# RMSNorm on one core: four of the first loads issued by ScalarE instead of SyncE, and gamma loaded in one piece

## The chip, the cores and the metric

The kernel runs on one core of a Trainium2 chip. The metric is the device time of one execution in microseconds (us). The core has a matrix engine (TensorE), three engines for elementwise work (VectorE, ScalarE, GpSimd), SyncE, which here only issues transfers, and sixteen DMA engines that move data between the chip's main memory (HBM) and the on-chip memory (SBUF). An engine that issues a transfer puts it on its own DMA queue; the sixteen DMA engines then work through it. In the profile PE is TensorE, DVE VectorE, ACT ScalarE, POOL GpSimd and SP SyncE; a q behind the name means its instruction queue.

## The reference

Each of 16 x 1024 rows of 512 float32 numbers is divided by its root mean square and multiplied by a vector gamma.

```python
def reference(x, gamma):          # x: 16 x 1024 x 512, gamma: 512, float32
    eps = 1e-5
    rms = np.sqrt(np.mean(x ** 2, axis=-1, keepdims=True) + eps)
    return (x / rms * gamma).astype(np.float32)
```

33.5 MB are read and 33.5 MB written.

## The kernel before

The 16384 rows are cut into four tiles t = 0 to 3. A tile has 128 partitions of 32 rows each; one row of a partition is 2 KB, so one row index over all partitions is 256 KB. Three buffers of a whole tile, slot 0 to 2 (line 40), hold tiles 0, 1, 2 and again slot 0 for tile 3. Results are written over the inputs in the slot and stored from there.

The work goes by nine groups of rows (line 76), each with a count of rows that GpSimd takes. For a group, ScalarE squares the rows (line 96) and VectorE adds the squares along each row (line 97), in pieces of up to nine rows. ScalarE takes the root of the mean (line 102) and VectorE its reciprocal (line 103). Then ScalarE multiplies the rows by the reciprocal one at a time (line 118) and VectorE multiplies them all by gamma (line 122); GpSimd does both steps for its own rows (lines 109 and 110). The loop of line 168 issues the squares of the next group ahead of the scaling of this one.

Gamma is loaded as one row of 512 numbers into one partition (line 58) and spread over the 128 partitions by a matmul with a column of ones (line 66). VectorE reads the product from TensorE's memory (PSUM); ScalarE copies it to SBUF for GpSimd (line 167), once, behind the reciprocals of the first group.

The schedule is written out by hand: each engine executes its instructions in the order of the program. Before the change every transfer is issued by SyncE, and so stands in one queue. The order at the start is: row 0 of tile 0 (line 55), rows 1 to 7 (line 56), gamma in five pieces (lines 57 and 58), rows 8 to 15, rows 16 to 31 (lines 59 and 60), and rows 0 to 15 of tile 1 (line 61). All the other transfers are issued in `transfers` (line 129), each group's at the end of its turn of the loop, so a store there waits for VectorE's product with gamma and for GpSimd's. The first of these is the store of row 0 after the first group.

The first group is the seven rows 0 to 6, so the first Square needs the first two loads. Completion of transfers is signalled on eight semaphores that are used in turn: the ninth transfer waits until the first one has landed, the tenth until the second one has, and so on. Before the change, rows 0 to 15 of tile 1 are the tenth transfer, and wait for rows 1 to 7 of tile 0.

ScalarE's instructions begin with an alignment of its code (line 34, in the trace a branch), then the load of the table for Sqrt and one Sqrt of a small constant (line 72), and then the Square of the first group.

## Time and profile before

| | before |
|---|---|
| median of 3 runs | 161.44 us (161.40 to 161.46) |
| the profiled execution | 161.45 us |
| its span, from the first to the last instruction | 159.7 us |
| busy: VectorE, ScalarE, GpSimd, TensorE | 112.0, 107.8, 106.4, 2.0 us |
| bytes read and written | 33.56 and 33.55 MB |
| first Square (line 96) | starts at 8.19 us |
| last product with gamma (line 122) | 131.92 us, 7.09 us long |

The times inside the span count from its first instruction. A busy time is the sum of an engine's instructions, without its issues of transfers and its waits. "Landing" is the moment when a transfer's completion has been signalled. In the windows, a row gives the stretch and its length in us, then the busy time of PE, PEld, DVE, ACT and POOL with the number of instructions, the granted clock of TensorE, the mean busy share of the sixteen DMA engines and what they moved in GB/s; a packet counts in the stretch in which it starts, so a single short stretch can show more than the engines can move.

### The profile page before, as it was taken

The numbers are of one execution on the slowest core, as the hardware profiler recorded it, in microseconds if no ns is written. First come the engines' busy times: TensorE is split into PE (matmuls) and PEld (weight loads), VectorE is DVE, ScalarE is ACT, GpSimd is POOL, SyncE is SP. The second block draws the span as 40 slices with busy tenths as digits, with TensorE's granted clock in tenths as the row PEclk, the third lists the DMA queues.
The fourth block names the chain that finished last, engine by engine and source line by source line (L and its number), as shares of the span: only waits on it lengthen the run. The fifth ranks groups of instructions, "written<-read, shape, count | busy, mean of one in ns | idle before, by whom it ended". The sixth has DMA issues, their size and how long they took to land.

```text
span 159.7 us, 276 instructions
## 1 busy us (share of the span) xinstructions
PE 2.0 (1%) x2; PEld 0.5 (0%) x2; DVE 112.0 (70%) x39; ACT 107.8 (68%) x108; POOL 106.4 (67%) x24
## 2 busy tenths in 40 slices
PE   0050000000000000000000000000000000000000
PEld 0010000000000000000000000000000000000000
DVE  0018098899798999999999999999999009800000
ACT  3071967976999999999899999989960990000000
POOL 1000951994999599999999999999999990000000
DMA  5999999999989989898999999979996997999995
GB/s 190 424 435 464 460 394 435 355 458 451 460 378 543 401 345 460 378 517 345 443 468 394 460 394 525 509 318 445 509 517 263 525 460 328 394 435 484 394 419 238
DMA packets 2747, 67.12 MB, mean 420 GB/s; under 512 B 313, under 2 KB 314, under 8 KB 826
## 3 DMA queue, kind: packets, MB, share of 16 engines
q1 hardware_dynamic: 2746, 67.11, 98.2%
q14 instruction: 1, 0.01, 0.0%
HBM read 33.56 MB, written 33.55 MB: 420 GB/s over the span
## 4 chain that ended last, share of the span: by engine, by line
DVE 59%; ACT 22%; DMA 4%; ACTq 0%; issue 0%; SPq 0%
DVE ss L97 36%; DVE slot L122 23%; ACT slot L118 8%; ACT slot L96 7%; ACT sq_psum L96 6%; DMA slot<-in_x_dram 4%; DVE ss L103 1%; ACT ss L102 1%; ACTq L210 0%; ACT gamma_b L167 0%; SPq L45 0%; ACTq L96 0%
## 5 line engine op out<-in xcount | busy, mean ns | idle before, releaser
L109 POOL TENSOR_TENSOR slot<-slot,ss 128x3584 f32<-128x3584 f32 (+2 forms) x9 | 46.9, 5214 | 24.0 <-DVE ss L103 24.0
L110 POOL TENSOR_TENSOR slot<-slot,gamma_b 128x3584 f32<-128x3584 f32 (+2 forms) x9 | 59.2, 6582 | 0.7
L97 DVE TENSOR_REDUCE ss<-sq_psum 128x7 f32<-128x3584 f32 (+1 forms) x13 | 42.2, 3246 | 13.5 <-ACT sq_psum L96 13.5
L118 ACT ACTIVATE slot<-slot,ss 128x512 f32<-128x512 f32 x75 | 47.2, 706 | 4.7 <-DVE ss L103 4.7
L122 DVE TENSOR_TENSOR slot<-slot,gamma_psum 128x4608 f32<-128x4608 f32 (+2 forms) x9 | 41.3, 4590 | 8.7 <-ACT slot L118 8.7
L96 ACT ACTIVATE sq_psum<-slot 128x3584 f32<-128x3584 f32 (+1 forms) x13 | 34.5, 2656 | 6.2 <-DMA slot<-in_x_dram 5.5
L97 DVE TENSOR_REDUCE ss<-slot 128x9 f32<-128x4608 f32 x3 | 14.9, 4953 | 4.4 <-ACT slot L96 4.2
L97 DVE TENSOR_REDUCE ss<-sq_sbuf 128x5 f32<-128x2560 f32 x5 | 14.0, 2801 | 0.0
L96 ACT ACTIVATE slot<-slot 128x4608 f32<-128x4608 f32 x3 | 12.1, 4033 | 0.0
L96 ACT ACTIVATE sq_sbuf<-slot 128x2560 f32<-128x2560 f32 x5 | 11.6, 2324 | 0.4 <-DMA slot<-in_x_dram 0.4
L102 ACT ACTIVATE ss<-ss,eps_t 128x16 f32<-128x16 f32 (+2 forms) x9 | 2.7, 304 | 11.6 <-DVE ss L97 11.6
L103 DVE RECIPROCAL ss<-ss 128x16 f32<-128x16 f32 (+2 forms) x9 | 2.1, 235 | 0.4 <-ACT ss L102 0.4
L66 PE MATMUL gamma_psum<-gamma_row,ones_col 1*128 1x512 f32 x2 | 2.0, 1122 | 8.7 <-DMA gamma_row<-in_gamma_dram 8.7
L72 ACT ACT_TABLE_LOAD x1 | 1.3, 1283 | 1.2 <-PEq L199 1.2
L167 ACT COPY gamma_b<-gamma_psum 128x512 f32<-128x512 f32 x1 | 0.6, 567 | 0.0
L66 PEld LDWEIGHTS gamma_psum<-gamma_row,ones_col 1*128 1x128 f32 x2 | 0.5, 304 | 8.7 <-issue 8.7
L64 POOL MEMSET ones_col<- 1x128 f32 x1 | 0.2, 194 | 0.3 <-POOLq L199 0.3
L199 POOL MEMSET const-float32-0.0<- 128x1 f32 x1 | 0.1, 99 | 0.2 <-issue 0.2
L72 ACT ACTIVATE table<-eps_t 128x1 f32<-128x1 f32 x1 | 0.2, 202 | 0.0
L199 POOL MEMSET const-bfloat16-1.0<- 128x1 bf16 x1 | 0.1, 102 | 0.0
L199 POOL MEMSET const-uint8-127<- 128x1 uint8 x1 | 0.1, 102 | 0.0
L199 POOL MEMSET const-float32-1.0<- 128x1 f32 x1 | 0.1, 99 | 0.0
(1 smaller groups left out, 0.1 us busy)
## 6 DMA issues: line engine op xcount, KB each, us to landing
slot<-in_x_dram SPq DMA_DIRECT2D x5, 4096.0 KB, 24.7
out_dram<-slot SPq DMA_DIRECT2D x3, 4096.0 KB, 20.3
out_dram<-slot SPq DMA_DIRECT2D x1, 7936.0 KB
slot<-in_x_dram SPq DMA_DIRECT2D x1, 5888.0 KB
out_dram<-slot SPq DMA_DIRECT2D x1, 3584.0 KB
slot<-in_x_dram SPq DMA_DIRECT2D x1, 2304.0 KB, 25.8
slot<-in_x_dram SPq DMA_DIRECT2D x1, 2048.0 KB, 9.8
slot<-in_x_dram SPq DMA_DIRECT2D x1, 1792.0 KB, 6.9
```

What stands on the lines that cost most here:

```text
L66: nc.tensor.matmul(gamma_psum[:, 0], ones_col, gamma_row, start=True, stop=True)
L72: nc.scalar.activation(out=table, in_=eps_t, func=AF.Sqrt)
L96: nc.scalar.activation(out=sq[:, :m], in_=rows, func=AF.Square)
L97: nc.vector.tensor_reduce(out=ss[:, r : r + m, 0], in_=sq[:, :m], axis=mybir.AxisListType.X, op=OP.add)
L102: nc.scalar.activation(out=ss[:, :n, 0], in_=ss[:, :n, 0], func=AF.Sqrt, bias=eps_t, scale=1.0 / D)
L103: nc.vector.reciprocal(out=ss[:, :n, 0], in_=ss[:, :n, 0])
L109: nc.gpsimd.tensor_tensor(out=part, in0=part, in1=by_row, op=OP.mult)
L110: last = nc.gpsimd.tensor_tensor(out=part, in0=part, in1=gamma_b.to_broadcast([P, share, D]), op=OP.mult)
L118: nc.scalar.activation(out=x[:, g + r, :], in_=x[:, g + r, :], func=AF.Copy, scale=rstd[:, r])
L122: scaled = nc.vector.tensor_tensor(out=part, in0=part, in1=gamma_psum.to_broadcast([P, r1 - r0, D]), op=OP.mult)
L167: nc.scalar.copy(out=gamma_b[:, 0], in_=gamma_psum[:, 0])
L199: nc = _bacc.Bacc("TRN2", target_bir_lowering=False, num_devices=1)
```

## The change

The load of the first row stays on SyncE. Rows 1 to 7, 8 to 15 and 16 to 31 of tile 0 and rows 0 to 15 of tile 1 are issued by ScalarE on its own queue, in that order, behind the alignment of line 34 and ahead of its table load. Gamma is one transfer of 2 KB on SyncE, behind the first row. All later transfers, and all compute instructions, stay where they are. With four transfers fewer, the turn of the eight semaphores shifts for all the later ones.

```diff
-    def load(t, slot, r0, r1):
-        dma = nc.sync.dma_start(out=slots[slot][:, r0:r1], in_=xv[t][:, r0:r1])
+    def load(t, slot, r0, r1, queue=nc.sync):
+        dma = queue.dma_start(out=slots[slot][:, r0:r1], in_=xv[t][:, r0:r1])
         before_scale.append((slot, r0, r1, dma))
...
     gamma_row = const.tile([1, D], fp32)
-    pieces = (0, 128, 224, 320, 416, D)
-
     load(0, 0, 0, 1)
-    load(0, 0, 1, 8)
-    for c0, c1 in zip(pieces, pieces[1:]):
-        nc.sync.dma_start(out=gamma_row[:, c0:c1], in_=gamma.unsqueeze(0)[:, c0:c1])
-    load(0, 0, 8, 16)
-    load(0, 0, 16, 32)
-    load(1, 1, 0, 16)
+    load(0, 0, 1, 8, nc.scalar)
+    nc.sync.dma_start(out=gamma_row, in_=gamma.unsqueeze(0))
+    load(0, 0, 8, 16, nc.scalar)
+    load(0, 0, 16, 32, nc.scalar)
+    load(1, 1, 0, 16, nc.scalar)
```

## The prediction, as it stood before the result

> **What bounds the kernel now.** I read the page's DMA rows first, then the chain, then SyncE's timeline, and last the DMA issues one at a time, because the first two rows contradict each other. The chain of the page:

> ```profile
> DVE 59%; ACT 22%; DMA 4%; ACTq 0%; issue 0%; SPq 0%
> ```

> By this the end is set by VectorE and ScalarE. But the DMA rows of the same page say that the transfers had no time left over:

> ```profile
> DMA  5999999999989989898999999979996997999995
> ...
> q1 hardware_dynamic: 2746, 67.11, 98.2%
> ...
> HBM read 33.56 MB, written 33.55 MB: 420 GB/s over the span
> ```

> All 67.11 MB go through one queue, and its packets took 98.2% of the sixteen engines' span. Whether the chain or the queue sets the end is told by SyncE's timeline, which lists when each transfer was issued:

> ```profile
> 0.74 0.86 SPq L45 DMA_DIRECT2D slot<-in_x_dram  x2
> 1.65 1.48 SPq L58 DMA_DIRECT2D gamma_row<-in_gamma_dram  x5
> 3.17 5.28 SPq L45 DMA_DIRECT2D slot<-in_x_dram  x3
> 27.23 0.35 SPq L49 DMA_DIRECT2D out_dram<-slot  x1
> ...
> 83.50 55.90 SPq L49 DMA_DIRECT2D out_dram<-slot  x4
> ```

> and by the DMA issues of single stretches (around 1.2, 8.1 and 139.1 us), each with its size and its time from issue to landing:

> ```profile
> slot<-in_x_dram SPq DMA_DIRECT2D x1, 1792.0 KB, 6.9
> ```
> ```profile
> slot<-in_x_dram SPq DMA_DIRECT2D x1, 4096.0 KB, 24.7
> ```
> ```profile
> out_dram<-slot SPq DMA_DIRECT2D x1, 4096.0 KB, 19.8
> ```

> The last one is the last store, issued at 139.1 when VectorE ended; it lands 19.8 us later. Its 4.19 MB need 9.8 us at the 426 GB/s that the windows give for 8 us to the end. So some 10 us of other transfers were still ahead of it: VectorE could have ended up to about 9 us later without moving the end. The chain only follows the last issue back to whoever released it and doesn't see the transfers queued ahead. The same holds at every place where SyncE waits for compute. The tightest is the first: the store issued at 27.23 finds ahead of it the load that was issued at 8.1 and lands 24.7 us later, at 32.8, so with the 1.0 us from an issue to its first bytes (first issue 0.74; the window 0 to 1.75 moved nothing) it came some 4.5 us early. **The end is set by the start of the first transfer plus 67.11 MB at the rate of the queue.** Only three things can move it: when the bytes start, how full the engines are in the first microseconds, and the rate. The windows show the start:

> ```profile
> 0.00:1.75 1.75, 0.00 (x0) 0.00 (x0) 0.00 (x0) 0.59 (x1) 0.43 (x6) 1.00 0.00 0
> 1.75:4.00 2.25, 0.00 (x0) 0.00 (x0) 0.00 (x0) 0.89 (x2) 0.00 (x0) 1.00 1.02 337
> 4.00:8.00 4.00, 0.00 (x0) 0.00 (x0) 0.00 (x0) 0.00 (x0) 0.00 (x0) 1.00 1.01 423
> 8.00:159.70 151.70, 2.04 (x2) 0.49 (x2) 112.04 (x39) 106.32 (x106) 105.95 (x18) 1.00 0.99 426
> ```

> The last two columns are the DMA share and GB/s: nothing until 1.75, 337 GB/s until 4.0, from there 423 to 426. The loss in the ramp is 2.25 x (1 - 337/426) = 0.47 us.

> The sum is made against the profiled execution's own 161.45 us: a span of 159.7 and 1.75 around it. The median of the runs is 161.44, so nothing need be corrected. A measurement of this kernel can tell about 0.2%, 0.32 us, from no change.

> **The change, part by part.** I call the five loads L1 (one row, 256 KB), L2 (seven rows), L3, L4 and L5.

> *L1 stays first on SyncE*: same place, 0.74. Its first bytes still come at 1.75. Cost 0.

> *L2 moves to ScalarE.* Before, SyncE issued it second: a first issue of 0.38 us (the chain's piece at 0.74), so L2 stood at 1.18. Now it is ScalarE's first work, behind the branch of line 34 that aligns its code. How early ScalarE can issue is read from its timeline:

> ```profile
> 1.16 1.28 ACT L72 ACT_TABLE_LOAD   x1 [1.16 <-PEq L199]
> ```

> ScalarE's first instruction behind that branch stands at 1.16 though the branch itself is at 0.73 and 33 ns long. In the built order of the changed kernel the four DMA copies stand behind the branch and ahead of this table load, so L2's issue takes its slot: 1.16 in place of 1.18, a gain of 0.02 us. Bounds: no earlier than 0.74 (SyncE's first issue after the same barrier), which would be 0.44 earlier; at the late end behind something as long as the table load, at 2.45. I take 1.16, since it is the same slot on the same engine.
> [...]

> But even an earlier L2 gains only what the engines are idle. L1's 256 KB take 0.62 us at 426 GB/s, so from 1.75 it keeps them busy until at least 2.37; L2 is needed there, which with 1.0 us from issue to bytes means an issue by 1.36. At 1.16 it has 0.2 us to spare. What L2 can do if it comes in beside L1 is fill the ramp: at most the 0.47 us above, at least nothing. I take 0.03: an L2 that is as early as before finds the same ramp.

> *L3, L4 and L5* follow on ScalarE, at 0.37 us each (the median of the ten issues of line 45, 0.33 to 0.60), about 1.6, 2.0 and 2.5. Before: 3.17, 3.66 and 8.1, the last of them held until L2 had landed, by the turn of eight DMA semaphores. They queue behind L2, which lands at 8.1, so an earlier issue moves no byte: 0.

> *ScalarE's compute behind them*: four issues of about 0.43 with their gaps put the table load at 2.9 in place of 1.16, its end and the small Sqrt at 4.4. The first Square waits for L1 and L2 until 8.19, which hides 3.8 us; even with all four at 0.60 it is hidden. If that cover were gone, each microsecond would delay the first store, which has its 4.5 us: 0.

> *SyncE*: one gamma issue for five saves some 1.2 us of an engine that then waits until 27.2: 0. Gamma lands earlier, TensorE's matmul (8.70) may start earlier, but the copy of its result stands at 15.52 behind VectorE's sums: 0. On the DMA engines gamma is 2 KB of 67 MB. The turn of semaphores shifts by four; each later issue of SyncE then waits on transfers that had landed at least 9 us before by the order of the queue, or on the same data as before: 0.

> *Two queues beside each other.* From 28.2 to 32.8 SyncE's store and loads run beside the rest of L5 on ScalarE's queue, where before they stood behind it. The bytes are the same. If the two share evenly, L5 lands between 32.8 and 37.4 (twice the 4.6 us left); its first reader, the Square at 37.69, takes it either way. Whether the rate changes is not shown by a one-queue trace: the window 28 to 32 has 349 GB/s against 426 in the 14 us before, some 0.7 us short, and the 22 us after it have 453 and pay it back. So between a gain and a loss of 0.7; I take 0, the rate over both stretches (437).

> Sum: 161.45 - 0.02 - 0.03 = **161.4 us**.

> **The rivals.**
> *Faster: the ramp is filled.* ScalarE issues L2 nearer to 0.74 and its long packets keep the engines full while L1's short ones start. For it: both engines pass the barrier together, and 337 GB/s is well below 426. Against it: 1.16, and L1's bytes are in the way. All of the ramp gives 161.45 - 0.47 = 161.0; it counts as faster from two thirds on.

> *Slower: L2 comes late.* It is ScalarE's first DMA, right behind a branch after which its next instruction took 0.39 us to come (0.76 to 1.16). If the first issue costs such a stop once more (1.55) and takes 0.60, the longest issue of line 45, in place of 0.38, it is 0.39 + 0.22 = 0.61 later. The engines run dry from a delay of 0.2 on (1.16 to 1.36), and each microsecond beyond costs one: 161.45 + 0.41 = 161.9. At the far end (2.45) it is 1.1, 162.5. For it: ScalarE has issued no DMA in this trace, so its price is unknown. Against it: four or five slots of SyncE, all under 0.6.

> *Slower as well, less likely: the shared stretch.* Two queues lower the rate at 28 to 33 by up to 0.7: 162.1. And the same with the other sign, 160.8.

> That the change doesn't do what it says is excluded: the built order shows the four copies ahead of ScalarE's table load, and a single gamma transfer.

> **How the numbers follow.** No change, 161.4, has 0.62: the end hangs on bytes, and none is added or taken away. Its own range is 161.13 to 161.76. The faster cases have 0.18 (ramp 0.13, shared stretch 0.05), the slower ones 0.20 (late L2 0.14, shared stretch 0.06). The range of 8 in 10 takes in the ramp rival and the late L2 at 0.41, and leaves out the far ends: 160.95 to 162.0.

> **What would show it.** L2's issue on ScalarE's queue near 1.16, and 337 GB/s or so in 1.75 to 4.0: step right; an issue at 0.8 and over 400 GB/s is the ramp rival, an issue after 1.4 and a hole in the window 2 to 3 the late one. The table load near 2.9 with the first Square still near 8.2; L5 landing before 37.4; the last store still landing some 19 us after an issue near 139. What would make it wrong: a DMA share well under 98%, or a last store that finds the queue empty, since then the chain and not the queue would set the end.

## The result and the profile after

The changed kernel takes **163.37 us** (median of 4 runs, 163.27 to 163.46) against 161.44: a ratio of 1.0103 over the runs that were compared (95% interval 1.0069 to 1.0138; the two medians alone give 1.0120). I had forecast 161.4 with a range up to 162.0. The profiled execution takes 163.30 with a span of 161.5, that is 1.85 more than that of the kernel before.

The loss sits at both ends of the span. First the start, in the timeline of the changed kernel (start, length, engine and line, what):

```profile
0.73 0.38 SPq L45 DMA_DIRECT2D slot<-in_x_dram  x1
...
1.17 0.31 SPq L55 DMA_DIRECT2D gamma_row<-in_gamma_dram  x1
1.17 3.73 ACTq L45 DMA_DIRECT2D slot<-in_x_dram  x4
3.28 0.50 PEld L63 LDWEIGHTS gamma_psum<-gamma_row,ones_col 1*128 1x128 f32 x2 [3.28 <-issue]
...
4.93 1.28 ACT L69 ACT_TABLE_LOAD   x1 [4.93 <-issue]
6.22 0.20 ACT L69 ACTIVATE table<-eps_t 128x1 f32<-128x1 f32 x1
9.71 3.16 ACT L93 ACTIVATE sq_psum<-slot 128x3584 f32<-128x3584 f32 x1 [3.28 <-DMA slot<-in_x_dram]
```

ScalarE starts to issue at 1.17, as forecast, but its four issues take 3.73 us and not 1.7. The answer for line 45 alone (shortest, median and longest in ns) says which:

```profile
L45 SPq DMA_DIRECT2D slot<-in_x_dram x6: 328/401/570, 0.7 to 77.7; - x6
L45 ACTq DMA_DIRECT2D slot<-in_x_dram x4: 448/506/2182, 1.2 to 4.3; - x4
```

One issue took 2182 ns, and the trace shows it to be the first, L2, from 1.17 to 3.35. With the 0.63 us from the end of an issue to its first bytes (before: 1.12 to 1.75) L2's bytes begin at 3.98. L1's end at 3.18, so the sixteen engines run empty. The windows of the changed kernel show it against 337 and 423 GB/s before:

```profile
1.75:4.00 2.25, 0.69 (x1) 0.50 (x2) 0.00 (x0) 0.00 (x0) 0.00 (x0) 1.00 0.51 133
4.00:8.00 4.00, 1.36 (x2) 0.00 (x0) 0.00 (x0) 1.49 (x2) 0.00 (x0) 1.00 0.98 355
8.00:28.00 20.00, 0.00 (x0) 0.00 (x0) 10.52 (x4) 11.76 (x10) 6.19 (x2) 1.00 1.02 439
```

2.25 x (337 - 133) + 4 x (423 - 355) = 731 KB fewer, 1.7 us at 426 GB/s (the bins count a packet where it starts, so this is good to a tenth or two). By the column with the DMA share, 2.25 x (1.02 - 0.51) + 4 x (1.01 - 0.98) = 1.27 us of it are engines that stand idle. The rest is a second ramp: from 4 to 8 us they are as busy as before, at 355 GB/s. From 8 us on the rate is what it was (438 before), and every later landing is 1.6 later: L5 at 34.4 in place of 32.8, the last store at 140.6 + 19.8 = 160.4 in place of 139.07 + 19.8 = 158.9:

```profile
out_dram<-slot SPq DMA_DIRECT2D x1, 4096.0 KB, 19.8
```

The other 0.25 us lie behind the last landing, in SyncE's checks of the semaphores. The same answer for the last line of the program, before and after:

```profile
L210 SPq EVENT_SEMAPHORE  x7: 17/28/28, 139.5 to 159.6; - x7
```
```profile
L207 SPq EVENT_SEMAPHORE  x7: 17/28/28, 160.5 to 161.5; - x7
```

Before, SyncE made its first checks at 139.5, while the last store was still moving, and the last of the five at 158.86 was the one that waited for it. After, the first check is the one that waits (until 160.45), and the other four follow behind the last landing, 62 ns apart. From the last landing to the end of the span it is 1.08 us in place of 0.83. So 1.60 + 0.25 = 1.85, all of the difference.

The rest went as forecast: two queues appear, and gamma's matmul starts at 3.3 in place of 8.7 without effect.

```profile
q1 hardware_dynamic: 2162, 54.79, 79.0%
q10 hardware_dynamic: 576, 12.32, 18.3%
```

### The profile page after: what moved, and what is told of

It reads as the page before. It is cut to its first block, busy times and chain, and to the rows that moved or that the text cites. A ratio compares the mean times of both kernels' runs of the same rounds, so it can differ in the third digit from the quotient of the medians.

```text
span 161.5 us, 270 instructions
## 1 busy us (share of the span) xinstructions
PE 2.0 (1%) x2; PEld 0.5 (0%) x2; DVE 112.0 (69%) x39; ACT 107.8 (67%) x108; POOL 106.4 (66%) x24
## 3 DMA queue, kind: packets, MB, share of 16 engines
HBM read 33.56 MB, written 33.55 MB: 416 GB/s over the span
## 4 chain that ended last, share of the span: by engine, by line
DVE 58%; ACT 22%; DMA 5%; issue 0%; ACTq 0%
DVE ss L94 35%; DVE slot L119 23%; ACT slot L115 8%; ACT slot L93 7%; ACT sq_psum L93 6%; DMA slot<-in_x_dram 5%; DVE ss L100 1%; ACT ss L99 1%; ACTq L207 0%; ACT gamma_b L164 0%; ACTq L34 0%
## 5 line engine op out<-in xcount | busy, mean ns | idle before, releaser
L93 ACT ACTIVATE sq_psum<-slot 128x3584 f32<-128x3584 f32 (+1 forms) x13 | 34.5, 2657 | 3.9 <-DMA slot<-in_x_dram 3.3
## 6 DMA issues: line engine op xcount, KB each, us to landing
slot<-in_x_dram SPq DMA_DIRECT2D x3, 4096.0 KB, 24.9
out_dram<-slot SPq DMA_DIRECT2D x3, 4096.0 KB, 20.4
slot<-in_x_dram ACTq DMA_DIRECT2D x2, 4096.0 KB, 25.2
```

What stands on the lines that cost most here:

```text
L93: nc.scalar.activation(out=sq[:, :m], in_=rows, func=AF.Square)
```

## The experiments

Theory: the first issue by ScalarE is slow, which empties the engines, and the turn of the semaphores leaves four more checks behind the last landing. Open at first were why that issue is slow, and how much of the loss is the queue's start and how much the first Square, 1.5 us later. The runs of some kernels spread over 2 us, as do a few of the kernel before (161.34 to 163.72 in these comparisons); where that matters I say where most lie.

**e1, L2 back on SyncE.**

```diff
-    load(0, 0, 1, 8, nc.scalar)
+    load(0, 0, 1, 8)
```

> The changed kernel, with the second load (rows 1 to 7) back on SyncE; the next three loads stay on ScalarE, gamma stays one piece. Theory 'first issue': ScalarE's first issue of a transfer takes 2.2 us whatever it carries, and cost the changed kernel its start because the second load hung on it. Here it falls on the load of rows 8 to 15, whose bytes are not wanted before 7.3, so the start is as before (first Square near 8.2) and only the end's 0.25 stays: 161.45 + 0.25 = 161.7. Rival 'two queues': the rate falls while two queues share the engines; then most of the loss stays, about 163. Rival 'shape': the seven-row load is slow to issue on ScalarE; then ScalarE's first issue is about 0.45 here, and the time 161.7 too.

Median 163.13, ratio 1.0052 (1.0010 to 1.0093). Five of twelve runs lie at 161.8 to 162.0, the others at 163.0 to 163.8 but for one at 165.0, and the profile (163.81) is one of those. Its first ScalarE issue, now L3, takes 2237 ns again, so it is not the shape of L2. Its start is not quite that of before: L3 shares the engines with L2 from 4.0 on, so L2 lands at 9.65 and the first Square starts at 9.74. The lower group fits the theory. In the profile of the upper one SyncE's issue behind the first store is long, and at 32.5 only 8 of the 16 engines are busy; e14 to e16 look into this. The group may not be e1's alone: 7 of the 23 runs of the kernel before beside it lie at 162.3 to 163.3 too, and none of those was traced.

```profile
29.19 2.81 SPq L45 DMA_DIRECT2D slot<-in_x_dram  x1
```

**e2, gamma in one piece, all on SyncE.**

```diff
-    for c0, c1 in zip(pieces, pieces[1:]):
-        nc.sync.dma_start(out=gamma_row[:, c0:c1], in_=gamma.unsqueeze(0)[:, c0:c1])
+    nc.sync.dma_start(out=gamma_row, in_=gamma.unsqueeze(0))
```

> The kernel before, all loads on SyncE, with gamma in one piece in place of five. Theory 'last check': with 20 transfers in place of 24 the last store uses another one of the eight semaphores, the one that SyncE checks first at the end, and the four checks behind it, 62 ns each in the changed kernel, come after the last landing in place of before: 161.45 + 0.25 = 161.70. Rival: gamma's pieces don't matter, 161.45; or the earlier issue of rows 0 to 15 of tile 1 (2.5 in place of 8.1) costs something at the start, seen as a later first Square.

Median 161.68 (all but two of the runs 161.57 to 161.83), ratio 0.9991 (0.9959 to 1.0022): by the ratio no difference can be told. The trace tells it: last landing at 158.76, end of the span 1.08 later, as in the changed kernel. All seven semaphore instructions stand behind the landing:

```profile
L208 SPq EVENT_SEMAPHORE  x7: 17/28/28, 158.8 to 159.8; - x7
```

So five pieces of gamma did one thing that shows: they made the last store the 24th transfer, on the semaphore that is checked last.

**e3, the changed kernel with gamma in five pieces.** The diff is e2's in reverse, on the changed kernel.

> The changed kernel with gamma in five pieces again, so that there are 24 transfers. Theory 'last check': the last store is again checked last, 163.30 - 0.25 = 163.05. Rival 'late start alone': no effect, 163.3.

Median 165.17, ratio 1.0199 (1.0158 to 1.0241): a miss. The end is 0.83 as the theory says, but with 24 transfers ScalarE itself has to wait, its third load for L2's landing (issue at 9.98), ahead of the table load and the first Square, which starts at 12.2. The first store comes at 31.25, and the issue behind it is long:

```profile
31.25 0.38 SPq L49 DMA_DIRECT2D out_dram<-slot  x1
31.67 2.39 SPq L45 DMA_DIRECT2D slot<-in_x_dram  x1
```

**e4, the table load ahead of the loads.** The four lines move up from behind the matmul.

```diff
+    eps_t = const.tile([P, 1], fp32)
+    nc.gpsimd.memset(eps_t, eps)
+    table = const.tile([P, 1], fp32)
+    nc.scalar.activation(out=table, in_=eps_t, func=AF.Sqrt)
     load(0, 0, 1, 8, nc.scalar)
```

> The changed kernel with ScalarE's table load and small Sqrt ahead of its four loads, so that its first issue stands at about 2.66 in place of 1.17. Theory 'first issue': it takes 2.2 us there too, the second load's bytes come 1.5 later: 163.3 + 1.5 = 164.8. Rival 'collision': the 2.2 us come from what happens between 1.2 and 2.4 (SyncE issuing beside it, the fetch of code behind the branch); then the issue takes 0.45 at 2.66, the bytes come about 0.25 earlier than in the changed kernel: 163.05.

Median 163.55, ratio 1.0101 (1.0050 to 1.0153). Neither: the issue didn't wait for the table load, but ran beside it.

```profile
1.19 1.28 ACT L57 ACT_TABLE_LOAD   x1 [1.19 <-PEq L196]
1.25 2.15 ACTq L45 DMA_DIRECT2D slot<-in_x_dram  x1
```

It started 0.08 later than in the changed kernel and ended 0.05 later, at 3.40. The test didn't move what it was to move.

**e5, all five loads and gamma by ScalarE.** Every `load` of the start, and gamma behind them, with `nc.scalar`.

> All five first loads and gamma by ScalarE, in the order row 0, rows 1 to 7, 8 to 15, 16 to 31, tile 1, gamma; SyncE issues nothing before the first store. Theory 'first issue': the first one, now the load of row 0, takes 2.2 us from 1.17, the first bytes come at 4.0 in place of 1.75, and the ramp behind them is that of the kernel before: 161.45 + 2.2 + 0.25 at the end = 163.9. Rival 'collision with SyncE's issues': nothing else issues, so the first issue takes 0.45 and the first bytes come at 2.2: 162.1.

Median 180.87, ratio 1.1191 (1.1169 to 1.1212). The first issue takes 2.35 us with nothing issued beside it, so it isn't a collision with SyncE. The time is another thing, which I had missed: gamma, last in ScalarE's queue, lands with the end of L5 (34.5), the matmul starts at 34.6, and the copy of gamma for GpSimd (at 36.7) holds up ScalarE. That is the price of a 2 KB transfer behind 12.6 MB.

**e6, no alignment.**

```diff
-    nc.scalar.addr_align(128, offset=0, max_nops=0)
```

> The changed kernel without the alignment of ScalarE's code (line 34), so without the branch ahead of its first issue. Theory 'first issue': it starts at 0.74 and takes 2.2 us, so the second load comes 0.43 earlier: 162.9. Rival 'fetch': the long issue is the fetch of code behind the branch; then it takes 0.4 to 0.5, the second load comes 2 us earlier, the start is as before or better: 161.3 to 161.7.

Median 161.84 (161.73 to 162.06), ratio 1.0002 (0.9975 to 1.0029). The first issue takes 415 ns, from 0.73:

```profile
L44 ACTq DMA_DIRECT2D slot<-in_x_dram x4: 415/454/508, 0.7 to 2.1; - x4
```

The answers on DMA for the stretch 1.5 to 2.5 tell what else went with the branch. The changed kernel has an 8 KB fetch of code there (1.80 to 2.43 in the trace), e6 has none; its only one comes at 63.4:

```profile
q1 hardware_dynamic: 49, 0.10, 55.7%
q14 instruction: 1, 0.01, 3.9%
```
```profile
q1 hardware_dynamic: 32, 0.07, 66.7%
q10 hardware_dynamic: 2, 0.03, 16.4%
```

**e7, gamma as ScalarE's first transfer.** Gamma's line with `nc.scalar`, ahead of L2.

> The changed kernel with gamma (2 KB) as ScalarE's first transfer in place of SyncE's second one, ahead of its four loads. Theory 'first issue': gamma takes the 2.2 us, the seven-row load behind it 0.45, its bytes come 0.45 later: 163.75. Rival 'shape': gamma takes 0.3, the seven-row load 2.2, 163.6; the times hardly differ, the durations of the two issues do.

Median 164.00, ratio 1.0177 (1.0126 to 1.0229). Gamma's issue takes 2.40 us, L2's behind it 0.37. The price hangs on the place, not on what is moved.

```profile
1.16 2.40 ACTq L54 DMA_DIRECT2D gamma_row<-in_gamma_dram  x1
3.60 1.90 ACTq L45 DMA_DIRECT2D slot<-in_x_dram  x4
```

**e8, e1 with one more load by ScalarE, in `transfers`.**

```diff
-            load(1, 1, 16, 32)
+            load(1, 1, 16, 32, nc.scalar)
```

> The kernel of e1 (second load on SyncE) with the load of rows 16 to 31 of tile 1 by ScalarE too, behind the first group's scaling, some 20 us after its last issue. Theory 'first issue': only the first issue of the execution takes 2.2 us; this one takes 0.35 to 0.6, and the time is that of e1, 161.7. Rival 'cold again': a queue left alone for 20 us takes 2.2 us again; ScalarE is 1.7 us later for the second group, which the 4.5 us of slack hide, the time is 161.7 as well: the duration of the issue tells.

Median 161.95, ratio 1.0014 (0.9986 to 1.0041). The late issue, at 17.0, takes 334 ns, so 12 us of rest don't bring the price back. And here none of the ten runs lies above 162.14: with that load queued early, behind L5 on ScalarE's queue, e1's upper group is gone. That is a hint and no proof, since e8 ran on another chip than e1.

**e9, the alignment behind the four loads.** The line of e6's diff moved to behind the load of tile 1.

> The changed kernel with the alignment of ScalarE's code behind its four loads instead of ahead of them. In the changed kernel the first issue took 2.18 us and in the kernel without the alignment 0.42, with an 8 KB fetch of code at 1.8 in the one and none there in the other. Theory 'fetch behind the branch': the first issue starts near 0.73 and takes 0.42, the fetch and the wait for it come behind the loads and are hidden under ScalarE's wait for the second load; the time is that of the kernel without the alignment: 161.45 + 0.25 (the end's checks) + 0.1 = 161.8. Rival 'layout': the aligned place of the later code is what costs; then 163.3.

Median 162.34, ratio 1.0033 (0.9998 to 1.0068); six of twelve runs at 161.73 to 162.13, the rest up to 163.7 (five of the 24 runs of the kernel before beside it are above 162.1 too). The first issue takes 402 ns, with the branch now at 2.72 and the fetch at 6.8: the aligned layout isn't what costs. In the profiled run (163.22) one DMA engine falls behind: from the load that lands near 103 on, its part comes 1.5 us after the other fifteen (102.95 against 101.49); why is open.

**e11, the first issue made to wait.**

```diff
+    nc.gpsimd.memset(slots[0][:, 1:8], 0.0)
     load(0, 0, 1, 8, nc.scalar)
```

> The changed kernel with a memset by GpSimd of the seven rows that ScalarE's first load fills, so that this load's issue waits for GpSimd (the load overwrites what the memset wrote). The alignment stays ahead. Theory 'fetch in flight': the 2.18 us are the time until the fetch of code behind the branch has come, near 3.4; an issue that starts later than that takes 0.4 to 0.5. Rival 'first issue behind the branch': it takes 2.2 us whenever it starts. The time follows GpSimd's memset, estimated at 2 to 4 us from 0.9: the second load comes at the earliest when it does in the changed kernel, so 163.3 or more.

Median 164.26, ratio 1.0172 (1.0112 to 1.0233). The branch is at 0.73 and the fetch at 1.88 to 2.41, as in the changed kernel; the memset ends at 3.82, the issue starts at 3.85 and takes **382 ns**.

```profile
L45 ACTq DMA_DIRECT2D slot<-in_x_dram x4: 382/452/533, 3.8 to 5.2; - x4
```

So it isn't the first issue as such, nor the first behind a branch: it is an issue close behind the branch, with the fetch on its way. In the seven traces in which that happened it ended 0.9 to 1.2 us after the fetch's packet, and 2.6 to 2.9 us behind the branch. That the issue waits for the fetch, and not for something else that the branch sets going, is the likeliest reading and not shown by itself: every trace with the branch has the fetch too.

**e10, e9 with gamma in five pieces.**

> The kernel of e9 with gamma in five pieces, so 24 transfers: both terms of the loss undone, with the loads still on ScalarE. ScalarE's third and fourth load now wait for the landing of the first two (near 8.2), so the first Square is some 2 us later, which the slack of 4.5 us before the first store takes. Theory 'two terms': 161.55. Rival, from the kernel with five pieces and the alignment ahead, whose second issue by SyncE took 2.4 us beside ScalarE's queue: the same stall comes back, 163.4. Either way the end, from the last landing to the last instruction, is 0.83 in place of 1.08.

Median 163.27, ratio 1.0092 (1.0061 to 1.0123): the rival. The end is 0.83, but ScalarE waits for L2's landing again (issue at 8.16), the first Square starts at 10.9, the first store comes at 29.9, and:

```profile
29.88 0.38 SPq L48 DMA_DIRECT2D out_dram<-slot  x1
30.30 2.03 SPq L44 DMA_DIRECT2D slot<-in_x_dram  x1
```

**e13, e6 with 24 transfers, without touching the start.**

```diff
-            store(1, 1, 1, 32)
+            for r0, r1 in ((1, 7), (7, 13), (13, 19), (19, 25), (25, 32)):
+                store(1, 1, r0, r1)
```

> The kernel of e6 (four loads on ScalarE, no alignment of its code) with the store of rows 1 to 31 of tile 1 cut into five, so that there are 24 transfers again without touching gamma or the start. The five are issued at 83.5 in 1.9 us, behind some 17 us of queued transfers. Theory 'two terms': start as in e6, the last store checked last, end 0.83 in place of 1.08: 161.84 - 0.25 = 161.6. Rival: the 0.25 is something else that two queues bring at the end, 161.84.

Median **161.69** (eleven of twelve at 161.53 to 161.84; the profiled run is the twelfth, at 162.8), ratio 1.0014 (0.9999 to 1.0029). The end is 0.83 again. With both terms undone and the four loads still on ScalarE, the time is that of the kernel before within what can be measured.

**e14, e15 and e16, a later first store on one queue.** The kernel before with more squares in the first group: all seven rows twice, or three or five of them once more.

```diff
         nc.scalar.activation(out=sq[:, :m], in_=rows, func=AF.Square)
+        if (t, g) == (0, 0):
+            nc.scalar.activation(out=sq[:, :3], in_=rows[:, :3], func=AF.Square)
```

> The kernel before, all loads on SyncE, with the first Square executed twice (the second overwrites the first with the same values), so that all compute of the first group and the first store come 3.1 us later: the store at 30.3 in place of 27.2, the queue being filled until 32.8. Theory 'slack' of the prediction: the end doesn't move, 161.45. Rival 'late second issue': as in e3 and e10, where SyncE's second issue came 2.0 to 2.4 us before ScalarE's last load had landed and took 2.0 to 2.4 us, SyncE's next issue stalls here too and the engines run dry: 163.3.

> The kernel before, with the Square of three of the first group's seven rows executed once more (same values), some 1.4 us: the first store at about 28.6 in place of 27.2, which is what the changed kernel's later first Square (9.71 in place of 8.19) did to it, but here with the queue unmoved. Theory 'the start of the queue': the changed kernel lost its 1.6 us to the engines' empty microseconds after 3.1 and not to the later compute; a store 1.4 later still finds the queue filled: 161.45. Rival 'the chain': there is no slack at all at this store, and the time is 162.9, so that the changed kernel's loss is the later Square by itself.

> The same with five rows, some 2.3 us: the first store at 29.5. e14 with 3.1 us cost 3.1. Theory 'the start of the queue' with a slack that ends somewhere between 1.4 and 3.1: anything from 161.45 to 163.0. Rival 'the chain': 163.7.

Medians 164.66, 161.97 and 163.40; ratios 1.0196 (1.0183 to 1.0209), 1.0032 (1.0020 to 1.0044) and 1.0101 (1.0075 to 1.0127). There is no second queue here, and no long issue:

```profile
30.43 0.35 SPq L49 DMA_DIRECT2D out_dram<-slot  x1
30.82 0.43 SPq L45 DMA_DIRECT2D slot<-in_x_dram  x1
```

In e14 the load issued at 30.82 reached the first engine at 32.05 and the last at 33.8, up to 3 us after its issue, while L5 had landed at 32.5. In the trace only 8 of the 16 engines were busy at 32.5. Over the runs the time goes with how long before L5's landing the first store is issued:

| | first store | L5 landed | ahead of it | time above the expected one |
|---|---|---|---|---|
| before | 27.2 | 32.8 | 5.6 | 0 |
| changed | 28.7 | 34.4 | 5.6 | 0 |
| e1 | 28.8 | 33.0 | 4.2 | 0.1 to 2.1 (one run 3.3) |
| e15 | 28.8 | 32.7 | 3.9 | 0.1 to 1.9, median 0.5 |
| e3 | 31.3 | 34.3 | 3.0 | 2.1 |
| e16 | 29.6 | 32.6 | 3.0 | 1.9 |
| e10 | 29.9 | 32.6 | 2.7 | 1.7 |
| e14 | 30.4 | 32.5 | 2.1 | 3.2 |

(The expected time is the forecast of each one's theory: 161.45 to 161.7, and 163.05 for e3; for the changed kernel it is the 163.3 that the late start and the end explain.) The changed kernel keeps its 5.6 us, since the queue and the store both moved, and in its trace all sixteen engines are busy from 4.5 us on. So its later Square cost nothing beyond the late start.

How a later store costs time is shown for e14 only. In the profiled runs of e15 (163.34) and e16 (163.40) most engines don't run dry behind the store: fifteen of the sixteen end the last store at 159.2 and 159.1 (before: 158.8), and one at 160.5 and 160.6. The profiled runs of e9 and e13 have such an engine as well, at 160.4 and 160.2 against 158.8 and 159.1, though their first stores came 5.6 us ahead. So a late first store isn't needed for one engine to fall behind, and why it does stays open.

**e12, one load of eight rows.**

```diff
-    load(0, 0, 0, 1)
-    load(0, 0, 1, 8)
+    load(0, 0, 0, 8)
```
and gamma in six pieces, which keeps 24 transfers.

> The kernel before, all on SyncE, with rows 0 to 7 of tile 0 as one load in place of one row and seven, and gamma in six pieces so that there are still 24 transfers. The first group needs seven rows anyway. If the ramp's 0.47 us (337 GB/s in 1.75 to 4.0) come from the short 2 KB packets of the first row, most of it is won: 161.1. Rival: the ramp is the start of the engines, whatever is moved: 161.4.

Median **161.35** (161.27 to 161.49) against 161.50 for the kernel before beside it, ratio 0.9972 (0.9946 to 0.9999): the one version ahead of both kernels, by 0.15 us, at the edge of what can be told. The rival holds for the ramp:

```profile
1.75:4.00 2.25, 0.00 (x0) 0.00 (x0) 0.00 (x0) 0.89 (x2) 0.00 (x0) 1.00 1.04 339
```

339 GB/s with long packets against 337: the ramp belongs to the start of the engines, not to the short packets.

## Why the prediction was wrong

**What bounds the kernel** was read rightly in the main: the loss is the empty time of the queue at the start, carried unchanged to the last landing, and the rate from 8 us on is the same. VectorE's order and durations did not change.

**The step that failed is "L2 moves to ScalarE".** I placed its issue at 1.16 and it started at 1.17; I gave it some 0.38 us and it took 2.18. The bound that I worked out, that the engines run dry if L2's issue comes after 1.36, held: the issue ended 1.76 later than one of 0.42 us from 1.17 would have; less the 0.2 us to spare that is 1.56, and the cost was 1.60. The rival "L2 comes late" had the place, and the suspicion of the branch, but its price was one more stop of 0.39 and an issue of 0.60; e6 and e11 show in its place an issue that the branch, most likely by its fetch of code, prolongs by some 1.8 us (2.18 in place of 0.42 and 0.38). I had read the 0.39 us from branch to table load as the whole price of the branch, because the only instruction that the trace of before had there was a table load, and that one doesn't wait (e4 shows both side by side: the table load from 1.19 takes the same 1.28 us, the issue from 1.25 takes 2.15). The trace of before has the same fetch, at 1.76 to 2.39, with no issue by ScalarE to meet it.

**"L2 earlier gains only what the engines are idle"** was right. In e6 L2 is issued at 0.73, 0.44 earlier than before, and the first Square starts at 8.22 (before 8.19). With e13 at 161.69 the 0.44 us bought nothing, since L1's bytes were in the way: from 1.75 to 4.00 the sixteen engines of e6 are busy as before (DMA share 0.99, before 1.02).

**The turn of semaphores** was costed at 0 with the waits of the later issues in mind. The trace of the kernel before has the landings of its 24 transfers on eight semaphores, three on each: L4, the ninth, is issued at 3.66 with L1 landed at 3.65, and L5, the tenth, at 8.12 with L2 landed at 8.10. Such waits were free in the changed kernel (not in e3 and e10, with 24 transfers), but I didn't follow the turn to the end of the program: 0.25 us, by e2 and the end of e13 (0.83) against e6 (1.08).

**The slack of 4.5 us** was wrong, though it didn't decide. A store 1.6 us later costs 0.1 to 1.9 (e15), 2.4 later 0.7 to 2.3 (e16), and 3.2 later all of the 3.2 (e14). In e14 the failing term is the 1.0 us from issue to bytes: it was the time of the first engine for a single transfer, where what must be in place is the load behind the store, in all sixteen engines, up to 3 us after its issue. What failed in e15 and e16 stays open, as said there.

**ScalarE's compute, SyncE's issues, gamma, and the shared stretch of two queues** were right at 0 in the changed kernel.

Open: why SyncE's second issue takes 2.0 to 2.8 us in e1, e3 and e10, where the queue is as short as in e16, which has no such issue. It ended within 0.4 us of the first engine's landing of L5 in all three. And why one engine falls behind in the profiled runs of e9, e13, e15 and e16.

## What to carry to other kernels

Where the DMA queue is full from start to end, look at the microseconds before it is full: in these runs an issue on another engine was worth there only what the DMA engines were idle (e6 and e13: L2 0.44 us earlier, and no gain), and cost what that engine did first (a branch and the long issue behind it, 1.60 us in the changed kernel), so look for a branch or an alignment of code ahead of it, and don't take its price from an instruction of another kind. Slack ahead of a queued transfer ended here well before the queue was empty: 5.4 to 5.6 us between the first store and the last landing ahead of it cost nothing in most runs, 3.9 us cost 0.5 in the median and 2.1 us cost 3.2. And the change in the number of transfers, 20 for 24, reached the end of the program through the semaphores, by 0.25 us: look that the last store is on the one that is checked last.
